# A new order of each engine's steps in a tuned f32 matrix product, with six sums a group on GpSimd where there were seven

## The chip, the cores and the metric

One core of a Trainium2 chip runs the whole program. The metric is the time of one execution on the device in microseconds; the profile is one profiled execution of the same program.

## The reference

```python
def reference(x, w):                     # x: 8 x 2048 x 2048, w: 2048 x 2048, float32
    cs = np.cumsum(x, axis=1)
    diff = cs - np.concatenate([zeros, cs[:, :-1, :]], axis=1)
    return np.matmul(diff, w).astype(np.float32)
```

The differences of a cumulated sum are the rows themselves, so the kernel computes x times w: 16384 x 2048 times 2048 x 2048.

## The kernel before

The 16384 rows are 128 row tiles of 128 rows. Each tile is loaded by SP in two halves into `F` (step `load`), its largest values are summed up by ScalarE (`weigh0`, `weigh1`, with an accumulator), GpSimd makes one number a row of it (`scale`, `unit`), VectorE the reciprocal (`recip`), ScalarE scales and narrows to fp16 (`narrow0`, `narrow1`), and SP turns it by DMA transposes (`turn0`, `turn1`) so that it can be TensorE's stationary operand. The weights stay in SBUF as fp16 blocks and differences of blocks.

The first 12 tiles go by separate code. The rest is 29 groups of four row tiles, g, h, k and l in the steps' names (tiles g, g+2, g+1, g+3). A group's product is a Strassen-Winograd scheme of two levels: seven products P1 to P7, of which P6 is done whole (eight parts `P6g.0` to `P6h.3`) and each other one is again seven quarters, `P1.p1` to `P1.p7`. A quarter is four matmuls of 128 x 128 by 128 x 512 into one PSUM bank; a group has 50 of them, 200 matmuls. Around them stand:

- large sums of row tiles on VectorE, 128 x 1024 fp16: `S1` to `S4` of each pair of tiles (`S1.g`, `S1.h` and so on);
- small sums, 128 x 512 fp16, four for each of P1, P2, P3, P4, P5 and P7: `P1.s1` to `P1.s4`, which feed p5, p6, p7 and p3. Those named in `ON_POOL` run on GpSimd, the others on VectorE;
- fills, 128 x 2048 fp16 on VectorE: differences of weights written into `flow` just before the quarter that uses them (`P1.fp4` before `P1.p4`, and so on; P7 has three);
- copies of PSUM banks to SBUF by ScalarE (`P1.cg`, `P1.ct`, `P7.c1` ...), sums of them back into banks by VectorE (`P1.m1`, `P7.a1`, `P7.a5g` ...), and the collection of results: `keep.C11g0` (ScalarE, the first part of a block of C into a buffer `c`), `add.C11g0.v` (VectorE, a further part added), `last.C12g0` (ScalarE, the scaling at the end), `put.C11g0` (SP, the store).

The order of it all is written out by hand in the string `ORDER`: some 270 steps, each with the number of groups it runs ahead. The loop at the end walks through it once for each group:

```python
for b in range(-early, len(groups) - late):
    for name, ahead in ORDER:
        if 0 <= b + ahead < len(groups):
            go_on(b + ahead, name)
```

Each engine issues its own steps in exactly this order (`after` chains them), and waits inside its queue for what a step needs from others. So the table fixes which step stands behind which on TensorE, VectorE, ScalarE, GpSimd and SP, and no step can overtake. SP's queue holds loads, turns and stores alike. In the last group the last quarters go by a table of their own (`END_ORDER`). In the first group P7 is done whole; `PLAINLY` says at which steps of the table its eight parts run. A few differences of weights that the scheme needs only once are made in the first group, at the steps named in `before`; `first(...)` is the one of its names that comes first.

Of the kernel before, what the change touches and what calls it, by code (L numbers as in the profile page):

```python
# [10 lines left out]
def kernel(  # L11
# [546 lines left out]

    def total(dst, p, q, op, pool=False):
        if pool:  # L560
            after("pool", lambda: nc.gpsimd.tensor_tensor(dst.all, p.all, q.all, op))  # L561
        else:
            after("dve", lambda: nc.vector.tensor_tensor(dst.all, p.all, q.all, op))  # L563
# [479 lines left out]

# [227 lines left out]
    ORDER = """
    P7.a5g+0 P7.p6+0 load.h+1 P7.c6+0 P7.p2+0 turn0.g+1 add.C22g0.x+0 keep.C12h1+0
    P5.p5+0 keep.C21g0+0 P7.a6+0 P5.s4+0 P3.s1+0 P7.p7+0 P7.c7+0 P4.p2+0 P7.a5h+0
    P3.s3+0 add.C21g0.x+0 narrow1.g+1 P5.p6+0 P7.a7h+0 P5.ct+0 put.C22g0+0 P3.p1+0
    weigh0.h+1 P5.m1+0 add.C12g0.q+0 weigh1.h+1 P7.p3+0 put.C21g0+0 P5.p7+0 P3.s2+0
    P3.s4+0 turn1.g+1 last.C12g0+0 P5.fp4+0 P5.m2+0 scale.h+1 recip.h+1 keep.C12h0+0
    unit.l+0 P5.p3+0 P3.p6+0 put.C12g0+0 P5.p4+0 P7.a7k+0 keep.C22g1+0 add.C22g1.x+0
    put.C22g1+0 P4.s2+0 P3.p3+0 P7.fp4+0 keep.C22h1+0 keep.C22h0+0 narrow0.h+1 load.k+1
    P4.s4+0 P4.p6+0 add.C12g1.z+0 P7.p4+0 add.C12h1.z+0 P3.p5+0 add.C22h1.x+0
    add.C12g1.q+0 add.C22h0.x+0 P4.p5+0 add.C12g1.e+0 P3.p4+0 P3.p7+0 keep.C21h1+0  # L1280
    narrow1.h+1 last.C12g1+0 P4.fp4+0 add.C12h0.z+0 add.C12h1.q+0 P4.s3+0 P4.p3+0
    add.C12h0.q+0 unit.g+1 add.C12h1.e+0 P2.p1+1 P1.p1+1 P4.p4+0 keep.C21g1+0 weigh0.k+1
    turn0.h+1 weigh1.k+1 scale.k+1 P1.s1+1 turn1.h+1 recip.k+1 P1.s3+1 P1.s2+1 unit.h+1
    add.C21g1.q+0 put.C12g1+0 last.C12h1+0 P1.cg+1 put.C22h0+0 P1.s4+1 P1.p5+1 P1.p6+1
    P2.s1+1 put.C22h1+0 put.C12h1+0 add.C21h1.e+0 narrow0.k+1 P1.ct+1 load.l+1 P1.m1+1
    last.C12h0+0 P4.p7+0 add.C21h1.q+0 P2.s2+1 narrow1.k+1 P1.p2+1 keep.C11g0+1
    turn1.k+1 P1.p7+1 P1.p3+1 keep.C21h0+0 unit.k+1 P2.cv+1 P1.fp4+1 P2.s4+1 P1.m2+1
    keep.C11g1+1 P2.p6+1 P1.p4+1 keep.C11h1+1 add.C21h0.x+0 P2.p5+1 add.C11g1.q+1
    P2.s3+1 weigh0.l+1 P2.fp4+1 turn0.k+1 add.C11h1.e+1 P2.p7+1 weigh1.l+1 scale.l+1
    put.C21h0+0 P2.p2+1 last.C21h1+0 recip.l+1 put.C12h0+0 add.C11h1.q+1 P2.p3+1 P2.p4+1  # L1290
    narrow0.l+1 add.C21g1.x+0 narrow1.l+1 put.C21h1+0 S1.g+1 keep.C11h0+1 S2.g+1
    add.C11g1.e+1 P5.p1+1 P5.cg+1 add.C11g0.v+1 P6g.1+1 turn0.l+1 P6g.2+1 P5.p2+1
    add.C11h0.q+1 turn1.l+1 load.g+2 S4.g+1 last.C21g1+0 P3.fp2+1 S1.h+1 P6g.3+1 P6g.0+1
    S2.h+1 last.C11h1+1 last.C11g1+1 P5.s1+1 keep.C22g0+1 weigh0.g+2 put.C21g1+0
    keep.C12g0+1 put.C11g0+1 put.C11h0+1 P5.s2+1 weigh1.g+2 P3.p2+1 P6h.2+1 scale.g+2
    P5.s3+1 S4.h+1 P6h.1+1 P7.fp5+1 S3.g+1 P6h.3+1 P6h.0+1 P4.s1+1 add.C12g0.z+1 S3.h+1
    keep.C12g1+1 P7.s1+1 P7.p1+1 put.C11h1+1 P7.s2+1 P4.p1+1 P7.c1+1 recip.g+2 P7.s3+1
    put.C11g1+1 P7.a1+1 P7.p5+1 P7.s4+1 narrow0.g+2 P7.fp7+1 P7.c5+1
    """
# [82 lines left out]
```

## Time and profile before

| what | us |
|---|---|
| median of 3 runs (lowest, highest) | 1457.22 (1456.07, 1460.31) |
| the profiled execution: its own time | 1458.12 |
| its span, first to last instruction | 1456.0 |
| TensorE busy in the span | 1430.1 (98%) |
| VectorE busy | 1391.5 (96%) |
| ScalarE busy | 1152.3 (79%) |
| GpSimd busy | 401.9 (28%) |
| mean granted TensorE clock | 1.000 |

The first 60 us load the weights, the 29 groups run from 171.2 us (the first matmul of group 0's `P1.p1`) to the end. The profile names lines, and most steps run through helpers: L592 is a quarter's matmuls, L573 those of a whole product, L563 a small or large sum on VectorE, L561 one on GpSimd, L958 a fill, L1055 and L1087 ScalarE's copies of banks, L1062 VectorE's sums into banks, L600 and L1117 `keep` and `last`, L603 and L1128 `add`, L614 `put`, L113 `load`, L185 `turn`, L125 `weigh`, L142 `scale`, L161 `unit`, L156 `recip`, L172 `narrow`. Which step a row is follows from its place in the order. A releaser in brackets is what ended the idle time before an instruction. TensorE's matmuls overlap in the rows: each is shown with 0.38 us, and in an unbroken run one starts 0.216 us after the other.

### The profile page before, as it was taken

What the parts mean: (1) busy time and instruction counts of PE and PEld (TensorE: products, weight loads), DVE (VectorE), ACT (ScalarE), POOL (GpSimd) and SP (SyncE); (2) the same over time, 40 slices, a digit from 0 to 9 for tenths busy, and PEclk for the clock granted to TensorE, in tenths of its full rate; (3) what the DMA queues carried; (4) which work ended last, traced back from release to release, by engine and by line L of the source; (5) the groups of instructions that cost most, each with busy time, mean ns of one, the idle gap of its engine ahead of it and who ended that gap; (6) DMA issues with size and microseconds to landing.
All of it is one profiled execution on the core that took longest, in us unless ns stands there. A gap on an engine that the chain in (4) does not pass through costs nothing. (4 is left out here: it accounts for less than half of the span.)

```text
span 1456.0 us, 21148 instructions
## 1 busy us (share of the span) xinstructions
PE 1430.1 (98%) x6561; PEld 637.2 (44%) x6567; DVE 1391.5 (96%) x2325; ACT 1152.3 (79%) x1782; POOL 401.9 (28%) x451
## 2 busy tenths in 40 slices
PE   8999999999999999999999999999999999999997
PEld 3444444444444444444444444444444444444443
DVE  7998879999999999999999999999999999999998
ACT  5887557888788888878888888888888888778882
POOL 0111122233232233232233232233232233232232
PEclk9999999999999999999999999999999999999999
DMA  9999849999889998899998889989889988899983
GB/s 355 365 243 301 209 144 229 257 229 249 219 237 245 241 234 254 234 232 251 234 238 248 236 241 256 237 232 252 237 240 250 242 226 249 233 233 256 237 235 122
DMA packets 377761, 351.65 MB, mean 242 GB/s; under 512 B 274800, under 2 KB 274800, under 8 KB 377520
## 3 DMA queue, kind: packets, MB, share of 16 engines
q1 hardware_dynamic: 377088, 348.47, 88.7%
q0 software_dynamic: 560, 1.84, 0.3%
q8 instruction: 51, 0.84, 0.3%
q14 instruction: 62, 0.51, 0.1%
HBM read 150.99 MB, written 134.22 MB: 196 GB/s over the span
## 5 line engine op out<-in xcount | busy, mean ns | idle before, releaser
L592 PE MATMUL b<-W,x 128*128 128x512 f16 x2116 | 509.8, 379 | 3.6 <-DVE x L563 1.2
L592 PEld LDWEIGHTS <-x 128*128 128x128 f16 x2936 | 285.4, 98 | 362.1 <-issue 18.7
L1128 DVE TENSOR_TENSOR c<-b,c 128x512 f32<-128x512 f32 x504 | 334.3, 689 | 4.5 <-PE b L592 3.6
L125 ACT ACTIVATE waste<-F 128x1024 uint8<-128x1024 f32 x246 | 260.7, 1060 | 94.8 <-DMA F<-in_x_dram 91.7
L592 PEld LDWEIGHTS <-inner 128*128 128x128 f16 x1984 | 192.1, 98 | 246.6 <-DVE inner L563 16.5
L592 PE MATMUL b<-W,inner 128*128 128x512 f16 x1168 | 295.0, 379 | 4.0 <-ACT c L1087 1.4
L172 ACT ACTIVATE F<-F,of 128x1024 f16<-128x1024 f32 x246 | 281.9, 1146 | 20.9 <-DVE of L156 19.0
L573 PE MATMUL b<-W,x 128*128 128x512 f16 x1248 | 285.7, 379 | 2.6 <-DVE x L563 2.3
L600 ACT ACTIVATE c<-b,of 128x512 f32<-128x512 f32 x268 | 176.2, 684 | 74.7 <-DMA out_dram<-c 42.9
L142 POOL TENSOR_SCALAR of<-of 128x1 f32<-128x1 f32 x112 | 59.9, 535 | 619.8 <-ACT waste L125 441.0
L603 DVE SCALAR_TENSOR_TENSOR c<-b,of,c 128x512 f32<-128x512 f32 x286 | 209.0, 746 | 10.3 <-PE b L592 4.2
L592 PE MATMUL b<-flow,x 128*128 128x512 f16 x812 | 208.3, 379 | 2.1 <-DVE of L156 1.1
L563 DVE TENSOR_TENSOR x<-x,x 128x1024 f16<-128x1024 f16 (+1 forms) x329 | 200.0, 616 | 7.7 <-DMA x<-F 4.9
L1062 DVE TENSOR_TENSOR b<-b,c 128x512 f32<-128x512 f32 x284 | 193.7, 694 | 7.9 <-ACT c L1087 3.4
L573 PEld LDWEIGHTS <-x 128*128 128x128 f16 x1248 | 121.5, 98 | 151.6 <-DVE x L563 7.8
L958 DVE TENSOR_TENSOR flow<-W 128x2048 f16<-128x2048 f16 x142 | 173.6, 1222 | 0.0
L600 ACT ACTIVATE c<-c,of 128x512 f32<-128x512 f32 x224 | 154.8, 715 | 10.1 <-DVE c L1128 7.7
L1117 ACT COPY c<-b 128x512 f32<-128x512 f32 x224 | 127.1, 581 | 18.3 <-DMA out_dram<-c 9.1
L561 POOL TENSOR_TENSOR x<-x,x 128x512 f16<-128x512 f16 x87 | 129.7, 1504 | 14.1 <-POOL x L561 7.6
L561 POOL TENSOR_TENSOR inner<-x,inner 128x512 f16<-128x512 f16 x58 | 95.7, 1651 | 118.3 <-PE b L592 118.3
L592 PE MATMUL b<-inner 128*128 128x512 f16 x472 | 121.1, 379 | 0.0
L561 POOL TENSOR_TENSOR inner<-inner,x 128x512 f16<-128x512 f16 x58 | 68.4, 1180 | 139.3 <-PE b L592 133.1
(77 smaller groups left out, 945.9 us busy)
## 6 DMA issues: line engine op xcount, KB each, us to landing
F<-in_x_dram SPq DMA_DIRECT2D x246, 512.0 KB, 5.7
out_dram<-c SPq DMA_DIRECT2D x492, 256.0 KB, 3.3
W<-in_w_dram SPq DMA_DIRECT2D x32, 512.0 KB, 9.5
W<-in_x_dram SPq DMA_DIRECT2D x16, 256.0 KB, 7.7
x<-F SPq DMA_TRANSPOSE x246, 3.6
out_dram<-o POOLq DMA_DIRECT2D x5, 256.0 KB, 4.0
out_dram<-o SPq DMA_DIRECT2D x5, 256.0 KB, 3.5
xP<-in_x_dram SPq DMA_DIRECT2D x1, 1024.0 KB, 5.4
```

The costliest lines, as they stand in the source:

```text
L125: lambda: nc.scalar.activation(waste, where[t][i], ABS, scale=1.0 / ROW, accum_out=sums_of[t][:, i : i + 1],),
L172: lambda: nc.scalar.activation(narrowed(t)[:, ds(i * NH, NH)], where[t][i], COPY, scale=s),
L561: after("pool", lambda: nc.gpsimd.tensor_tensor(dst.all, p.all, q.all, op))
L563: after("dve", lambda: nc.vector.tensor_tensor(dst.all, p.all, q.all, op))
L573: said = nc.tensor.matmul(to[n], a[k], b[k][:, n, :], start=(first and k == 0), stop=(k == KH - 1), skip_group_check=True,)
L592: said = nc.tensor.matmul(to, a[k], b[k], start=(first and k == 0), stop=(k == 3), skip_group_check=True)
L600: after("act", lambda: nc.scalar.activation(c, p, COPY, scale=u))
L603: after("dve", lambda: nc.vector.scalar_tensor_tensor(c, p, u, c, MUL, ADD))
L958: after("dve", lambda: nc.vector.tensor_tensor(in_twos(flow), x, y, op))
L1062: after("dve", lambda: nc.vector.tensor_tensor(t, p, s, ADD))
L1117: after("act", lambda: nc.scalar.copy(to, p))
L1128: after("dve", lambda: nc.vector.tensor_tensor(to, p, to, ADD))
```

## The change

Three things change: the table `ORDER`, the list of small sums that run on GpSimd, and the places of the first group's P7.

```diff
-    ON_POOL = "P2.s2 P2.s4 P3.s2 P4.s2 P4.s3 P4.s4 P5.s4".split()
+    ON_POOL = "P3.s1 P4.s2 P4.s3 P4.s4 P5.s3 P5.s4".split()
...
     ORDER = """
-    P7.a5g+0 P7.p6+0 load.h+1 P7.c6+0 P7.p2+0 turn0.g+1 add.C22g0.x+0 keep.C12h1+0
...
+    P6h.1+0 P6h.3+0 keep.C12g0+0 P5.s3+0 add.C12g0.z+0 put.C11h1+0 weigh0.g+1 weigh1.g+1
...
     PLAINLY = {
-        "P7.p1": ["P7g.0"],
-        "P7.p5": ["P7g.1"],
-        "P7.p6": ["P7g.2"],
-        "P7.p2": ["P7g.3"],
+        "P7.p2": ["P7g.0", "P7g.1", "P7g.2", "P7g.3"],
         "P7.a7k": ["P7h.0", "P7h.1"],
-        "P7.fp4": ["P7h.2"],
-        "P7.p4": ["P7h.3"],
+        "P7.fp4": ["P7h.2", "P7h.3"],
     }
```

The set of steps is the same. P2.s2, P2.s4 and P3.s2 move from GpSimd to VectorE, P3.s1 and P5.s3 from VectorE to GpSimd. On TensorE four quarters now stand between `P1.p1` and `P1.p5` (`P4.p5`, `P4.p3` and `P4.p4` of the group before, and `P2.p1`), where `P4.p4` alone stood. The three places that the prediction speaks of most, in the middle of the program:

VectorE around `S3.h`, before. Tiles x00 and x01 are the two halves of tile g, x10 and x11 of h, x20 and x21 of k, x30 and x31 of l. The rows are S3.g, P4.s1, add.C12g0.z, S3.h, P7.s1, P7.s2, recip.g, P7.s3 and P7.a1:

```order
L563 TENSOR_TENSOR x00_63<-x21_68,x00_63 128x1024
L563 TENSOR_TENSOR x20_67<-x31_70 128x512
L1128 TENSOR_TENSOR c5_767<-b7_791,c5_767 128x512
L563 TENSOR_TENSOR x10_65<-x31_70,x10_65 128x1024
L563 TENSOR_TENSOR inner_779<-x10_65 128x512
L563 TENSOR_TENSOR inner_779<-inner_779,x00_63 128x512
L156 RECIPROCAL of_6472<-of_6472 128x1
L563 TENSOR_TENSOR x10_65<-x00_63,x10_65 128x512
L1062 TENSOR_TENSOR b2_786<-b2_786,c4_763 128x512
```

and now, from S2.h and S3.g on: add.C11h0.q, add.C12g0.z, P5.s2, S4.h, P7.fp5, S3.h, recip.g, P7.s1, P4.s1, P7.s2:

```order
L563 TENSOR_TENSOR x10_65<-x30_69,x10_65 128x1024
L563 TENSOR_TENSOR x00_63<-x21_68,x00_63 128x1024
L603 SCALAR_TENSOR_TENSOR c2_755<-b7_791,of_6185,c2_755 128x512
L1128 TENSOR_TENSOR c0_747<-b5_789,c0_747 128x512
L563 TENSOR_TENSOR inner_779<-inner_779,x20_67 128x512
L563 TENSOR_TENSOR x11_66<-x11_66,x10_65 128x1024
L958 TENSOR_TENSOR flow_783<-W_58 128x2048
L563 TENSOR_TENSOR x10_65<-x31_70,x10_65 128x1024
L156 RECIPROCAL of_6499<-of_6499 128x1
L563 TENSOR_TENSOR inner_779<-x10_65 128x512
L563 TENSOR_TENSOR x20_67<-x31_70 128x512
L563 TENSOR_TENSOR inner_779<-inner_779,x00_63 128x512
```

The reciprocal of the next tile g stands ahead of P7.s1 and P7.s2 and no longer behind them; S3.g stands ahead of S4.h and the fill P7.fp5; P7.s2 is no longer right behind P7.s1, and P5.s3 has left for GpSimd.

SP behind the turns of tile l (x30, x31), before:

```order
L185 DMA_TRANSPOSE x30_69<-F_62 128x8x128
L185 DMA_TRANSPOSE x31_70<-F_62 128x8x128
L113 DMA F_62<-in_x_dram 128x1024 x2
L614 DMA out_0_dram<-c1_751 128x512
L614 DMA out_0_dram<-c4_763 128x512
```

and now:

```order
L185 DMA_TRANSPOSE x30_69<-F_62 128x8x128
L185 DMA_TRANSPOSE x31_70<-F_62 128x8x128
L614 DMA out_0_dram<-c4_763 128x512
L113 DMA F_62<-in_x_dram 128x1024 x2
L614 DMA out_0_dram<-c6_771 128x512
```

A store (put.C21h0 of the group before) now stands between the second turn and load.g.

GpSimd in one group, before: P2.s2, unit, P2.s4, two scales, P5.s4, P3.s2, scale, unit, P4.s2, P4.s4, P4.s3:

```order
L561 TENSOR_TENSOR inner_779<-inner_779,x01_64 128x512
L161 TENSOR_SCALAR of_3333<-of_3333,uw_59 128x1
L561 TENSOR_TENSOR inner_779<-x01_64,inner_779 128x512
L142 TENSOR_SCALAR of_3412<-of_3412 128x1
L142 TENSOR_SCALAR of_3488<-of_3488 128x1
L561 TENSOR_TENSOR inner_779<-x20_67,inner_779 128x512
L561 TENSOR_TENSOR inner_779<-inner_779,x01_64 128x512
L142 TENSOR_SCALAR of_3596<-of_3596 128x1
L161 TENSOR_SCALAR of_3412<-of_3412,uw_59 128x1
L561 TENSOR_TENSOR x20_67<-x20_67,x21_68 128x512
L561 TENSOR_TENSOR x30_69<-x21_68,x20_67 128x512
L561 TENSOR_TENSOR x31_70<-x21_68,x31_70 128x512
```

and now, from P5.s3 on: scale, P5.s4, P3.s1, P4.s2, scale, P4.s4, P4.s3:

```order
L561 TENSOR_TENSOR x30_69<-x20_67,x30_69 128x512
L142 TENSOR_SCALAR of_3888<-of_3888 128x1
L561 TENSOR_TENSOR inner_779<-x20_67,inner_779 128x512
L561 TENSOR_TENSOR inner_779<-x11_66 128x512
L561 TENSOR_TENSOR x20_67<-x20_67,x21_68 128x512
L142 TENSOR_SCALAR of_3947<-of_3947 128x1
L561 TENSOR_TENSOR x30_69<-x21_68,x20_67 128x512
L561 TENSOR_TENSOR x31_70<-x21_68,x31_70 128x512
```

The two sums of P2 are gone from it, P5.s3 has come ahead of scale.g, and P3.s1 takes the place of P3.s2.

More of the change, by code (lines that the diff above doesn't have):

```diff
@@ L1271 @@
     ORDER = """
-    P7.a5g+0 P7.p6+0 load.h+1 P7.c6+0 P7.p2+0 turn0.g+1 add.C22g0.x+0 keep.C12h1+0
[L1273 to L1295, printed above, removed]
@@ L1296 @@
-    P5.s3+1 S4.h+1 P6h.1+1 P7.fp5+1 S3.g+1 P6h.3+1 P6h.0+1 P4.s1+1 add.C12g0.z+1 S3.h+1
-    keep.C12g1+1 P7.s1+1 P7.p1+1 put.C11h1+1 P7.s2+1 P4.p1+1 P7.c1+1 recip.g+2 P7.s3+1
-    put.C11g1+1 P7.a1+1 P7.p5+1 P7.s4+1 narrow0.g+2 P7.fp7+1 P7.c5+1
+    P6h.1+0 P6h.3+0 keep.C12g0+0 P5.s3+0 add.C12g0.z+0 put.C11h1+0 weigh0.g+1 weigh1.g+1
+    put.C11g1+0 scale.g+1 P5.s2+0 P7.p1+0 S4.h+0 P7.c1+0 P7.fp5+0 S3.h+0 recip.g+1
+    P7.s1+0 P4.s1+0 narrow0.g+1 P7.s2+0 P7.s3+0 P4.p1+0 put.C11g0+0 P7.a1+0 P7.p5+0
@@ new lines @@
+    P7.s4+0 P7.fp7+0 P7.p6+0 keep.C12g1+0 put.C11h0+0 P7.c5+0 P7.p2+0 P5.p5+0 P7.a5g+0
+    P7.c6+0 add.C22g0.x+0 keep.C12h1+0 P7.a5h+0 P7.a6+0 P7.p7+0 load.h+1 weigh0.h+1
+    P7.c7+0 put.C22g0+0 P7.a7h+0 P4.p2+0 keep.C21g0+0 P5.s4+0 P5.p6+0 add.C21g0.x+0
+    P5.ct+0 P3.s1+0 P5.m1+0 P7.p3+0 turn0.g+1 P3.p1+0 P5.p3+0 P4.s2+0 narrow1.g+1
+    P5.p7+0 P3.s2+0 P3.s3+0 weigh1.h+1 P4.p6+0 scale.h+1 P3.s4+0 keep.C22g1+0
+    add.C12g0.q+0 P5.fp4+0 put.C21g0+0 P3.p3+0 P5.m2+0 add.C22g1.x+0 keep.C12h0+0
@@ new lines @@
+    P7.a7k+0 P5.p4+0 add.C12g1.z+0 P3.p6+0 last.C12g0+0 keep.C22h0+0 recip.h+1 P3.p5+0
+    keep.C22h1+0 P7.fp4+0 P4.s4+0 add.C12g1.q+0 P3.p4+0 turn1.g+1 put.C12g0+0
+    add.C22h1.x+0 narrow0.h+1 add.C12g1.e+0 keep.C21h1+0 put.C22g1+0 add.C12h1.e+0
+    P7.p4+0 P4.s3+0 add.C22h0.x+0 load.k+1 P3.p7+0 turn0.h+1 P4.fp4+0 narrow1.h+1
+    last.C12g1+0 weigh0.k+1 weigh1.k+1 scale.k+1 P1.p1+1 unit.g+1 P4.p5+0 turn1.h+1
+    add.C12h1.z+0 P4.p3+0 add.C12h1.q+0 unit.h+1 P4.p4+0 add.C12h0.z+0 P2.p1+1
+    last.C12h1+0 P1.s1+1 put.C22h1+0 add.C12h0.q+0 P1.s2+1 keep.C21g1+0 P1.p5+1
@@ new lines @@
+    recip.k+1 put.C12g1+0 P2.s1+1 add.C21h1.e+0 put.C22h0+0 P1.cg+1 P1.s4+1 last.C12h0+0
+    P1.ct+1 P1.p6+1 add.C21g1.q+0 put.C12h1+0 load.l+1 narrow0.k+1 P1.m1+1 P1.p2+1
+    P4.p7+0 keep.C11g0+1 P1.s3+1 P2.s2+1 add.C21g1.x+0 add.C21h1.q+0 turn0.k+1 P1.fp4+1
+    narrow1.k+1 P1.p3+1 turn1.k+1 P2.s4+1 P2.cv+1 keep.C21h0+0 add.C21h0.x+0 P2.p6+1
+    P1.p7+1 P1.m2+1 P2.p2+1 P2.p5+1 weigh0.l+1 keep.C11g1+1 weigh1.l+1 scale.l+1
+    add.C11g1.q+1 P2.s3+1 put.C12h0+0 P1.p4+1 P2.p7+1 keep.C11h1+1 recip.l+1
@@ L1299 @@
+    add.C11h1.e+1 last.C21h1+0 P2.p3+1 S1.g+1 S2.g+1 unit.k+1 add.C11h1.q+1 P2.fp4+1
+    P5.p1+1 add.C11g1.e+1 put.C21h1+0 S4.g+1 narrow0.l+1 narrow1.l+1 P6g.1+1 P6g.0+1
+    P5.cg+1 turn0.l+1 keep.C11h0+1 P2.p4+1 last.C11h1+1 add.C11g0.v+1 last.C21g1+0
+    P5.p2+1 turn1.l+1 keep.C22g0+1 P6g.3+1 P3.fp2+1 put.C21h0+0 S1.h+1 load.g+2 P5.s1+1
+    S2.h+1 P6g.2+1 P3.p2+1 put.C21g1+0 last.C11g1+1 S3.g+1 add.C11h0.q+1 unit.l+1
+    P6h.2+1 P6h.0+1
     """
```

## The prediction

> **What bounds the kernel now.** I read the page's busy times first, then the windows cut at the starts of groups of four row tiles, then the waits of single engines, then the timeline of one undisturbed and one disturbed group.
>
> ```profile
> span 1456.0 us, 21148 instructions
> PE 1430.1 (98%) x6561; PEld 637.2 (44%) x6567; DVE 1391.5 (96%) x2325; ACT 1152.3 (79%) x1782; POOL 401.9 (28%) x451
> ...
> 171.20:217.30 46.10, 43.33 (x197) 18.90 (x196) 36.93 (x56) 23.66 (x38) 10.79 (x10) 1.00 0.57 163
> 217.30:263.10 45.80, 43.92 (x201) 19.32 (x200) 44.93 (x77) 36.50 (x59) 14.19 (x15) 1.00 0.92 230
> 263.10:1358.60 1095.50, 1089.51 (x5001) 485.76 (x5000) 1069.33 (x1827) 904.34 (x1427) 332.89 (x375) 1.00 0.91 240
> 791.10:920.80 129.70, 129.70 (x601) 58.62 (x600) 128.05 (x221) 108.70 (x171) 39.97 (x45) 1.00 0.90 244
> 834.40:877.60 43.20, 43.20 (x201) 19.51 (x200) 42.65 (x74) 36.18 (x58) 13.40 (x15) 1.00 0.91 244
> 659.40:703.60 44.20, 43.68 (x201) 19.25 (x200) 42.73 (x74) 36.26 (x57) 13.26 (x15) 1.00 0.93 235
> 1402.60:1456.00 53.40, 45.44 (x206) 19.78 (x204) 48.70 (x79) 26.09 (x40) 11.85 (x12) 0.99 0.54 164
> ```
>
> The columns of a window are its length, then the busy time of PE, PEld, DVE, ACT and POOL, the granted clock, the DMA share and GB/s. The group at 834.40 is the yardstick: TensorE never pauses, and 200 matmuls take 43.20 us, so one quarter (four matmuls) takes 0.864. VectorE works 42.65 of these 43.20 us, so it has 0.55 us to spare in a group. The window from 791.10 holds three such groups in a row; cut at their first matmuls in the timeline, 8 of 25 groups are within 0.15 us of this bare time. The 25 groups from 263.10 to 1358.60 take 1095.50 where 25 x 43.20 = 1080.0 would do: 15.5 us are lost, more than the busy column shows (1095.50 - 1089.51 = 6.0), since each pause is partly covered by the modelled end of the matmul before it. The first two groups lose 91.9 - 86.4 = 5.5 more. That is all an order can win in the steady part. In the last group VectorE is the longer queue (48.70 against 45.44).
>
> Who is late is told by VectorE's waits in those 25 groups:
>
> ```profile
> DVE of L156 <- POOL of L142: 6.9, 27, 0.7
> DVE x L563 <- DMA x<-F: 4.5, 7, 1.1
> DVE b L1062 <- ACT c L1087: 3.4, 7, 0.9
> DVE inner L563 <- DMA x<-F: 1.6, 5, 0.5
> ```
>
> They sum to 16.4 us, about the 15.5 lost. One case, in the group at 659.40, VectorE's row ahead of TensorE's:
>
> ```profile
> 677.68 1.42 DVE L563 TENSOR_TENSOR x<-x,x 128x1024 f16<-128x1024 f16 x2 [0.93 <-DMA x<-F]
> ...
> 679.16 3.63 PE L573 MATMUL b<-W,x 128*128 128x512 f16 x16 [0.43 <-DVE x L563]
> ```
>
> The transpose of tile l lands 0.93 late, S1.h waits, P6h waits for S2.h, and this group is 1.0 us longer than the yardstick. With so little idle time VectorE can't catch up within the group, so a late arrival is paid nearly in full.
>
> **The change, part by part.** *One more small sum on VectorE.* P2.s2, P2.s4 and P3.s2 come to VectorE, P3.s1 and P5.s3 leave it: seven GpSimd sums become six in each of 29 groups. The price is in these rows:
>
> ```profile
> 853.01 0.42 DVE L563 TENSOR_TENSOR inner<-x 128x512 f16<-128x512 f16 x1
> 853.46 0.42 DVE L563 TENSOR_TENSOR inner<-inner,x 128x512 f16<-128x512 f16 x1
> 853.80 1.02 DVE L563 TENSOR_TENSOR x<-x,x 128x512 f16<-128x512 f16 x2
> ```
>
> The third starts 0.34 after the second, which it doesn't read. The second, which reads the first's result, starts 0.45 after it. So an extra sum takes 0.34 of the queue, and a sum right behind its own source 0.11 more. Of such neighbours a group has five before (S2.g, S2.h, P5.s2, P7.s1, P7.s2) and three now (S2.g, P5.s1, C12h1.q): 0.34 - 2 x 0.11 = 0.12 a group. The spare 0.55 hides it in an undisturbed group. Where something is late it counts; with 25 - 8 = 17 groups longer than the yardstick I charge 17 x 0.12 = 2.0 us. If the cover were gone everywhere it would be 29 x 0.12 = 3.5.
>
> *GpSimd loses a sum.* It is busy 28%, and no wait of TensorE names it. Worth 0.
>
> *The order of TensorE's quarters.* P1.p5 now has four quarters between itself and P1.p1 (P4.p5, P4.p3, P4.p4, P2.p1) where it had one, so P1.s1 seems to have 2.6 us more time. But the three P4 quarters and P2.p1 came earlier before, and VectorE's P1.s1 stands behind the same additions. Against the total work done nothing moves: 0.
>
> *S3.g of the first group.* This group's P7 is a whole product, and its first part sat right behind P6h:
>
> ```profile
> 190.00 3.62 PE L573 MATMUL b<-W,x 128*128 128x512 f16 x16
> 194.53 1.04 PE L573 MATMUL b<-W,x 128*128 128x512 f16 x4 [0.91 <-DVE x L563]
> ```
>
> Sixteen matmuls from 190.00 end their issue at 193.46, so 1.07 us are lost waiting for S3.g. Now all four parts stand at P7.p2, behind P4.p1, and S3.g stands ahead of S4.h. I take 1.1 us as won (at least 0, if S3.g is as late as before; at most the 5.5 us of the first two groups).
>
> *recip.l and recip.k.* These are the 6.9 us in 27 waits above, 42% of all. recip.k now stands behind P1.s2 rather than directly behind P1.s1, and the loads that feed k come no later against it. If this kind goes, 42% of 15.5 = 6.5 us goes. The landings (4.5 + 1.6) have no more room than before: S1.h still follows the second turn of l with nothing but additions and one fill between. I leave them. Bounds for this term: 0 to 15.5; I take 6.5, less the 2.0 above.
>
> *recip.g in front of P7.s1, and a put in front of load.g.* This speaks against the change. Rows of the undisturbed group, by time:
>
> ```profile
> 849.51 1.01 SPq L113 DMA_DIRECT2D F<-in_x_dram  x2
> 850.57 3.37 SPq L614 DMA_DIRECT2D out_dram<-c  x5
> ...
> 856.23 1.06 ACT L125 ACTIVATE waste<-F 128x1024 uint8<-128x1024 f32 x1
> 857.47 0.78 POOL L142 TENSOR_SCALAR of<-of 128x1 f32<-128x1 f32 x1 [12.09 <-DMA out_dram<-c]
> 858.13 0.42 DVE L563 TENSOR_TENSOR inner<-x 128x512 f16<-128x512 f16 x1
> ...
> 858.61 1.53 PEld L592 LDWEIGHTS <-inner 128*128 128x128 f16 x8 [0.19 <-DVE inner L563]
> 858.93 0.16 DVE L156 RECIPROCAL of<-of 128x1 f32<-128x1 f32 x1
> ```
>
> load.g is issued at 849.51, weigh1.g waits for it, scale.g ends at 857.47 + 0.78 = 858.25, and P7.p5 starts at 858.61 behind P7.s1. Before, recip.g comes after P7.s1 and P7.s2, so it could be 0.7 late at no cost. Now it stands ahead of P7.s1, and P7.s1 has to start by 858.61 - 0.05 - 0.42 = 858.14, the reciprocal 0.08 earlier, at 858.06. P1.p5 to P7.p5 is 26 quarters in both orders, and ScalarE's queue from P1.ct to narrow1.l keeps its list but for one entry: narrow0.k now stands behind P1.ct, where last.C12h0 stood.
>
> ```profile
> 836.30 1.03 PE L592 MATMUL b<-W,inner 128*128 128x512 f16 x4
> ...
> 836.75 1.14 ACT L172 ACTIVATE F<-F,of 128x1024 f16<-128x1024 f32 x1
> 837.80 0.56 ACT L1055 COPY c<-b 128x512 f32<-128x512 f32 x1
> 838.26 0.72 ACT L600 ACTIVATE c<-c,of 128x512 f32<-128x512 f32 x1
> 838.89 1.13 ACT L172 ACTIVATE F<-F,of 128x1024 f16<-128x1024 f32 x1
> 839.93 1.24 ACT L600 ACTIVATE c<-b,of 128x512 f32<-128x512 f32 x2
> ```
>
> By the starts, narrow0.k (1.05) for last.C12h0 (0.63) makes the chain 0.42 longer; but P1.ct, which began at 837.80, need no longer wait for narrow0.k behind the end of P1.p5 at 837.33, 0.47 less. The two cancel. So scale.g is late by the 858.25 - 858.06 = 0.19, and by a put that now stands on SP between the second turn of l and load.g, 3.37 / 5 = 0.67: 0.86 us a group. Yet scale.g takes not 0.78 but on the mean of all its kind
>
> ```profile
> L142 POOL TENSOR_SCALAR of<-of 128x1 f32<-128x1 f32 x112 | 59.9, 535 | 619.8 <-ACT waste L125 441.0
> ```
>
> 0.535. Whether SP's issue or the data set load.g's landing the trace doesn't show (the DMA share is 0.91), so of the put's 0.67 I take the middle between none and all: 0.19 + 0.33 - 0.25 = 0.27. A group that is already late at an earlier place doesn't pay it again; I charge the eight groups at the bare time and as many that the recip term frees, 16 x 0.27 = 4.3 us. The bounds are 0 and 25 x 0.86 = 21.5.
>
> *GpSimd sums beside VectorE's f16 sums.* One collision is in the trace, in the last group:
>
> ```profile
> 1434.40 1.16 POOL L561 TENSOR_TENSOR x<-x,x 128x512 f16<-128x512 f16 x1
> 1434.92 0.92 DVE L563 TENSOR_TENSOR inner<-x,inner 128x512 f16<-128x512 f16 x1
> 1435.76 1.21 DVE L958 TENSOR_TENSOR flow<-W 128x2048 f16<-128x2048 f16 x1
> ```
>
> P3.s4 takes 0.92 instead of 0.42 while GpSimd's sum is under way. So a collision costs 0.50 and the kernel before has one; removing it wins 0.5 at most. The Trainium skill (SBUF — State Buffer, "Who interferes with whom") says that a VectorE instruction with two SBUF inputs and a GpSimd instruction that reads SBUF contend, and that whichever comes second waits for the whole of the first. The trace agrees here with 0.92; by that rule any new overlap would cost VectorE up to GpSimd's 1.16, and the sum would be 25 x 0.5 = 12.5 us worse if one arose in each group. I find no certain one in the new order and take 0; its upper end is a rival.
>
> *The tail.* VectorE's last group grows by 0.12 and nothing covers it: 0.1.
>
> **The sum.** -1.1 - 6.5 + 2.0 + 4.3 + 0.1 = -1.2 us. The profiled execution took 1458.12 (span 1456.0 and 2.1 around it), 0.9 above the median of 1457.22; so that execution would come to 1456.9, and the median to 1456.0. That is 0.1%, within the 0.3% (4.4 us) which a measurement of this kernel can just tell from no change.
>
> **Rivals.** *Most late arrivals are swallowed (faster).* In the new order P7.fp4 has three quarters between its release by P5.p4 and P7.p4 instead of two, and P5.m1 feeds P5.p3 only after two other quarters. If the chains have slack at most places, two thirds of 15.5 go, 10.3, with 1.1 of the start and no new price: 1457.2 - 11.4 = 1445.8. For it: eight groups already run at the bare 43.2, so no fixed term stands in the way. Against it: the landings depend on transfers whose DMA share is 0.91 in either order.
>
> *The recip.g chain binds in every group (slower).* Price 0.6 in all 25 groups instead of 0.27 in 16: 25 x 0.6 - 1.1 - 4.5 + 0.1 = +9.5, or 1466.7. It decides from (4.4 + 5.5) / 25 = 0.40 a group on. For it: the 0.78 of the undisturbed group, and 0.25 MB more queued ahead of load.g. Against: the mean of 0.535, and that late groups don't pay twice.
>
> *GpSimd's P5.s3 holds P5.s2 (slower).* P5.s3 may begin when S2.h ends, behind S3.g's reads, and P5.s2 follows on VectorE three steps after S3.g began, 1.8 us. GpSimd would need 0.6 of waiting and 1.16 of work, also 1.8. If it loses that race in each group: 25 x 0.5 - 1.1 - 4.5 + 0.1 = +7.0, or 1464.2. By the skill's rule above this race is real; the trace shows only the one collision.
>
> *It changes nothing.* The stated aim, no GpSimd sum just ahead of a small VectorE sum, already holds in 28 of 29 groups; a time equal to before lies inside my forecast.
>
> **How the numbers follow.** The forecast near no change 0.37 (its own range 1453 to 1461); swallowed arrivals 0.35; recip.g chain 0.18; GpSimd race 0.10. Hence faster 0.35, same 0.37, slower 0.28. The range goes from 1446, the time of the fast rival, to 1468, just past the slow one; the outer tails hold about 0.1 each.
>
> **What would show it.** Right: the window of 25 groups near 1091 to 1095; waits "DVE of L156 <- POOL of L142" below 6.9; the first PE pause at 194 gone; small sums beside GpSimd all at 0.42. Wrong on recip.g: that wait rises above 10 and sits ahead of an "inner<-x" sum, with TensorE pausing 0.3 or more at P7.p5 in most groups. Wrong on the race: VectorE f16 sums of 0.9. Wrong on the fast side: most groups at 43.2.

## The result: 2.7% slower, and the profile after

The changed kernel takes 1496.60 us (median of 4 runs, 1495.16 to 1499.30) against 1456.64 for the kernel before in the same runs: a ratio of 1.0272, 95% interval 1.0248 to 1.0296, or 40 us. The prediction said 1456.0 with a range up to 1468. It was wrong by far.

The page's head, and the windows cut at the first matmuls of P1.p1 (columns as in the prediction: length, PE, PEld, DVE, ACT, POOL, granted clock, DMA share, GB/s). The first two are the first two groups, then come the 25 groups from the third on, one group among them, and the last group:

```profile
span 1494.2 us, 21188 instructions
PE 1443.4 (97%) x6567; PEld 632.4 (42%) x6567; DVE 1412.6 (95%) x2354; ACT 1143.9 (77%) x1782; POOL 352.7 (24%) x422
...
170.17:217.84 47.67, 43.42 (x189) 18.56 (x188) 33.88 (x54) 21.12 (x35) 9.87 (x8) 0.96 0.56 156
217.84:264.89 47.05, 44.24 (x202) 19.23 (x200) 45.66 (x79) 36.89 (x59) 11.23 (x14) 1.00 0.81 217
264.89:1391.19 1126.30, 1099.48 (x5002) 480.82 (x5001) 1089.30 (x1849) 896.43 (x1425) 290.04 (x350) 1.00 0.85 234
895.04:940.46 45.42, 43.95 (x201) 19.23 (x200) 43.59 (x75) 35.82 (x58) 11.59 (x14) 1.00 0.82 231
1437.19:1494.20 57.01, 48.94 (x218) 20.77 (x216) 52.45 (x85) 29.03 (x46) 10.97 (x12) 0.99 0.52 158
```

The 25 groups take 1126.30 instead of 1095.50, so 30.8 of the span's 38.2 us (1494.2 - 1456.0) are lost there, 1.2 in each group. The shortest of them takes 44.5; none is near 43.2 any more. The first group's window holds 189 matmuls where it held 197 (the order moves two quarters behind the cut, 8 x 0.216 = 1.7 us), so like for like it is 3.3 us longer and not 1.6. The last group's 3.6 more are for the greater part no loss of their own: P1.p1 now stands three quarters (2.6 us) earlier in a group's work, so that work which used to lie ahead of the cut lies behind it.

VectorE's waits in these 25 groups, and its fills `flow<-W` there, after:

```profile
DVE of L156 <- POOL of L142: 30.7, 50, 2.1
DVE x L563 <- DMA x<-F: 1.7, 5, 0.5
```

```profile
L958 DVE TENSOR_TENSOR flow<-W 128x2048 f16<-128x2048 f16 x125 | 174.7, 1398 | 0.0
```

and the same fills in the 25 groups of the kernel before:

```profile
L958 DVE TENSOR_TENSOR flow<-W 128x2048 f16<-128x2048 f16 x125 | 152.8, 1223 | 0.0
```

Two prices stand out. VectorE waits 30.7 us for GpSimd's `scale` where it waited 6.9; by the rows 25.3 of these are recip.g, once in every group. And 125 fills take 21.9 us more, all of it in one of the five fills of a group. Together that is 45.7 us. The late turns and the copies of ScalarE that VectorE waited for before (4.5 + 1.6 + 3.4) have shrunk to 1.7, which leaves 38; the 7 us between this and the 30.8 are less than VectorE's former idle time of 0.55 a group, 25 x 0.55 = 13.8.

One group of the changed kernel by time. First around recip.g:

```profile
876.62 0.68 DVE L563 TENSOR_TENSOR x<-x,x 128x1024 f16<-128x1024 f16 x1
876.71 1.06 ACT L125 ACTIVATE waste<-F 128x1024 uint8<-128x1024 f32 x1 [0.56 <-DMA F<-in_x_dram]
877.96 0.30 POOL L142 TENSOR_SCALAR of<-of 128x1 f32<-128x1 f32 x1 [3.57 <-ACT waste L125]
878.29 0.16 DVE L156 RECIPROCAL of<-of 128x1 f32<-128x1 f32 x1 [0.98 <-POOL of L142]
878.37 0.41 DVE L563 TENSOR_TENSOR inner<-x 128x512 f16<-128x512 f16 x1
878.83 1.04 PE L592 MATMUL b<-flow,inner 128*128 128x512 f16 x4 [0.61 <-DVE inner L563]
```

S3.h ends at 877.30, and then VectorE stands still for 0.98 us: the half tile that ScalarE weighs (L125) landed only at 876.7, and GpSimd's `scale` follows the weighing. P7.s1 and with it TensorE's P7.p5 wait behind the reciprocal. Then the fill P7.fp4 of the same group, 12.97 us behind P7.s1:

```profile
891.24 3.25 POOL L561 TENSOR_TENSOR x<-x,x 128x512 f16<-128x512 f16 x2 [3.76 <-PE b L592]
891.34 2.14 DVE L958 TENSOR_TENSOR flow<-W 128x2048 f16<-128x2048 f16 x1
```

GpSimd's P4.s4 starts 0.10 ahead of it (the row joins P4.s4, 1.15 us, and P4.s3). The fill takes 2.14 instead of 1.22: the sum is done at 892.39, and the fill ends 1.09 behind it. The same pair in the kernel before, in the group that the prediction used as its yardstick:

```profile
870.35 2.25 POOL L561 TENSOR_TENSOR x<-x,x 128x512 f16<-128x512 f16 x1 [0.28 <-POOL x L561]
870.36 1.22 DVE L958 TENSOR_TENSOR flow<-W 128x2048 f16<-128x2048 f16 x1
```

Here they start 0.01 us apart, the fill has its usual 1.22, and it is GpSimd's sum that takes 2.25 instead of 1.16, where nobody waits for it. So the two collided in the kernel before as well. Which of them waits has changed.

### The profile page after: what moved, and what is told of

Same layout as the page of the kernel before. It is cut to its first block, busy times and chain, and to the rows that moved or that the text cites. A ratio compares the mean times of both kernels' runs of the same rounds, so it can differ in the third digit from the quotient of the medians.

```text
span 1494.2 us, 21188 instructions
## 1 busy us (share of the span) xinstructions
PE 1443.4 (97%) x6567; PEld 632.4 (42%) x6567; DVE 1412.6 (95%) x2354; ACT 1143.9 (77%) x1782; POOL 352.7 (24%) x422
## 4 chain that ended last, share of the span: by engine, by line
DVE 39%; DMA 17%; PE 17%; issue 13%; ACT 10%; SPq 2%; POOL 1%; DVEq 0%; ACTq 0%
DMA F<-in_x_dram 12%; DVE c L1128 12%; PE b L592 9%; DVE flow L958 8%; DVE b L1062 7%; PE b L573 6%; DVE c L603 5%; ACT waste L125 4%; DVE x L563 4%; DVE inner L563 3%; ACT F L172 2%; PE b L289 2%; ACT b L1055 2%; ACT c L600 1%; DMA out_dram<-c 1%
## 5 line engine op out<-in xcount | busy, mean ns | idle before, releaser
L592 PE MATMUL b<-W,x 128*128 128x512 f16 x2116 | 518.6, 379 | 3.9 <-DVE c L603 2.0
L125 ACT ACTIVATE waste<-F 128x1024 uint8<-128x1024 f32 x246 | 260.7, 1060 | 69.8 <-DMA F<-in_x_dram 68.1
L592 PEld LDWEIGHTS <-inner 128*128 128x128 f16 x1984 | 186.7, 98 | 291.2 <-DVE inner L563 73.4
L573 PE MATMUL b<-W,x 128*128 128x512 f16 x1248 | 287.3, 381 | 3.8 <-ACT c L1117 2.6
L561 POOL TENSOR_TENSOR x<-x,x 128x512 f16<-128x512 f16 x116 | 170.9, 1484 | 365.0 <-DVE x L563 229.5
L958 DVE TENSOR_TENSOR flow<-W 128x2048 f16<-128x2048 f16 x142 | 196.7, 1385 | 0.0
L563 DVE TENSOR_TENSOR x<-x,x 128x1024 f16<-128x1024 f16 (+1 forms) x300 | 187.6, 633 | 3.1 <-DMA x<-F 1.7
L1117 ACT COPY c<-b 128x512 f32<-128x512 f32 x224 | 130.4, 583 | 45.0 <-DVE c L603 33.2
L142 POOL TENSOR_SCALAR of<-of 128x1 f32<-128x1 f32 x112 | 38.0, 339 | 536.4 <-ACT waste L125 536.4
L600 ACT ACTIVATE c<-c,of 128x512 f32<-128x512 f32 x224 | 159.3, 724 | 1.1 <-DVE c L1128 1.1
L592 PE MATMUL b<-inner 128*128 128x512 f16 x472 | 116.6, 379 | 0.0
L1055 ACT COPY b<-b 128x512 f32<-128x512 f32 x87 | 50.4, 579 | 66.4 <-DVE c L1128 62.0
L1087 ACT COPY c<-b 128x512 f32<-128x512 f32 x112 | 65.4, 585 | 24.7 <-PE b L592 23.4
```

Of the source, the lines that this page charges most:

```text
L125: lambda: nc.scalar.activation(waste, where[t][i], ABS, scale=1.0 / ROW, accum_out=sums_of[t][:, i : i + 1],),
L573: said = nc.tensor.matmul(to[n], a[k], b[k][:, n, :], start=(first and k == 0), stop=(k == KH - 1), skip_group_check=True,)
L592: said = nc.tensor.matmul(to, a[k], b[k], start=(first and k == 0), stop=(k == 3), skip_group_check=True)
L600: after("act", lambda: nc.scalar.activation(c, p, COPY, scale=u))
L958: after("dve", lambda: nc.vector.tensor_tensor(in_twos(flow), x, y, op))
L1117: after("act", lambda: nc.scalar.copy(to, p))
```

## The experiments

Theory: two prices on VectorE's queue, each paid in nearly every group. (a) A race: whichever of the fill and the GpSimd sum comes second waits for the first, and a few hundredths of a microsecond decide. (b) The chain from recip.l over the turns, the store put.C21h0 and load.g to recip.g is longer than VectorE's work between the two. Rivals: one price that causes the other, VectorE's longer queue alone, or transfers.

### The race, from both sides

In the changed kernel, `recip.h+1` moved from in front of `P7.fp4+0` to right behind it:

```diff
-    ... keep.C22h0+0 recip.h+1 P3.p5+0 keep.C22h1+0 P7.fp4+0 P4.s4+0 ...
+    ... keep.C22h0+0 P3.p5+0 keep.C22h1+0 P7.fp4+0 recip.h+1 P4.s4+0 ...
```

> The changed kernel with one reciprocal (recip.h, 0.08 us of VectorE's queue) moved from in front of the fill P7.fp4 to behind it; nothing else. Theory of the race: the fill then starts about 0.02 instead of 0.09 after GpSimd's P4.s4 and wins, as in the kernel before, where the offset is 0.01; the fill takes 1.22 instead of 2.14, P4.s4 takes 2.2 instead of 1.16, and the time falls by 27 x 0.92 = 25 us, to about 1472. If 0.02 is still too late, the fill stays at about 2.1 and the time at 1496. Rival, the fill is slow because of something other than who starts first: no change, 1495 to 1498.

Measured: 1480.79 us, 15.8 less, ratio to the kernel before 1.0163 (1.0143 to 1.0184). The pair now:

```profile
930.44 2.25 POOL L561 TENSOR_TENSOR x<-x,x 128x512 f16<-128x512 f16 x1 [3.77 <-PE b L592]
930.46 1.22 DVE L958 TENSOR_TENSOR flow<-W 128x2048 f16<-128x2048 f16 x1
```

An instruction of 0.08 us taken from in front of the fill hands the wait back to GpSimd in 23 of 25 groups. It won 16 us and not 25, since recip.g's waits grew (27.3 us in the 25 groups against 25.3) and late turns show again that lateness had covered (S1.g, S1.h and P1.s1 wait 6.3 us together, against 1.8).

The counterpart in the kernel before, one reciprocal too many in front of the fill:

```diff
+    spare = const.tile([P, 1], f32, name="spare")
...
+        if name == "P7.fp4" and groups[i].more:
+            after("dve", lambda: nc.vector.reciprocal(spare, uw))
```

> The kernel before with one extra reciprocal of 128 x 1 to a spare tile in front of the fill P7.fp4 in each steady group; its result is not used. It costs VectorE's queue 0.08 us a group by itself, at most 29 x 0.08 = 2.3 us. Theory of the race: the fill now starts 0.09 after GpSimd's P4.s4 instead of 0.01 and waits for it, 2.14 instead of 1.22; VectorE's queue grows from 42.7 to 43.7 us, over TensorE's 43.2, and a group that took 43.8 on the mean takes 44.3 to 44.8: 1470 to 1485. Rival, the fill's slowness belongs to the other order and not to who starts first: 1457 to 1459.

Measured: 1477.69 us against 1457.79 of the kernel before in the same runs, ratio 1.0142 (1.0125 to 1.0160). An extra instruction that costs 2.3 us at most by itself costs 20:

```profile
925.32 3.25 POOL L562 TENSOR_TENSOR x<-x,x 128x512 f16<-128x512 f16 x2 [0.29 <-POOL x L562]
925.33 0.15 DVE L1343 RECIPROCAL spare<-uw 128x1 f32<-128x1 f32 x1
925.40 2.15 DVE L959 TENSOR_TENSOR flow<-W 128x2048 f16<-128x2048 f16 x1
```

The order of the rest is that of the kernel before; only the start of the fill has moved by 0.08, and 22 of 25 fills are hit. TensorE pays at once, by 18.9 us of pauses in the 25 groups at P7.p4, the quarter that reads the fill. This settles (a).

### recip.g's chain

The reciprocal later, in the changed kernel (the narrowing that reads it goes behind P7.c5):

```diff
-    ... S3.h+0 recip.g+1 P7.s1+0 P4.s1+0 narrow0.g+1 P7.s2+0 P7.s3+0 P4.p1+0 ... P7.c5+0 P7.p2+0 ...
+    ... S3.h+0 P7.s1+0 P4.s1+0 P7.s2+0 P7.s3+0 recip.g+1 P4.p1+0 ... P7.c5+0 narrow0.g+1 P7.p2+0 ...
```

> The changed kernel with the reciprocal of the next tile g three small sums later on VectorE (behind P7.s3), and the narrowing that needs it behind P7.c5. Theory of two prices (the wait of recip.g and the fill P7.fp4 behind a GpSimd sum are paid one beside the other on VectorE's queue): the wait of about 1.02 us a group goes, the fill stays at 2.14, a group takes about 44.1 instead of 45.1, and the time is 1496.6 - 27 x 1.1 = about 1467. Rival, one price (the fill is hit only because the wait holds VectorE back against TensorE): the fill falls to 1.22 as well, groups go to 43.2 to 43.9, and the time is 1450 to 1460. Rival, the longer VectorE queue alone (42.82 us of work in 43.2): no gain over 5 us.

Measured: 1466.87 us, 29.7 less, ratio 1.0066 (1.0051 to 1.0081), as the theory of two prices had it. recip.g's waits in the 25 groups fall from 25.3 to 2.2 us, and the fill is still hit in 18 of 25: the race is a price of its own. Of the 29.7 us, 20.0 are won in the 25 groups; the first group falls from 47.7 to 43.6 us, of which more below.

What makes the chain long? put.C21h0 in front of the turns of l, where SP has time. The kernel before had it on that side of the turns too, further ahead:

```diff
-    P5.cg+1 turn0.l+1 ... P3.fp2+1 put.C21h0+0 S1.h+1 load.g+2
+    P5.cg+1 put.C21h0+0 turn0.l+1 ... P3.fp2+1 S1.h+1 load.g+2
```

> The changed kernel with the store put.C21h0 moved the other way on SP, in front of the two turns of l instead of between them and load.g, so that load.g follows the second turn directly and no buffer comes free later. If the store's issue of 0.6 to 0.67 us stands in the chain that ends in recip.g, the wait of recip.g falls from 1.0 to about 0.4 and the time to 1496.6 - 27 x 0.6 = about 1480. If load.g's landing is set by the data on their way, the wait stays at about 1.0 and the time at 1494 to 1498.

Measured: 1474.40 us, 22.2 less, ratio 1.0116 (1.0100 to 1.0131). VectorE's waits for `scale` over the whole program, first in this run, then in the changed kernel:

```profile
DVE of L156 <- POOL of L142: 12.7, 53, 0.9
```

```profile
DVE of L156 <- POOL of L142: 34.3, 55, 2.1
```

recip.g's part falls from 25.3 to 5.7 us in 25 groups, 0.8 a group; what stays is mostly 0.20 each. But the store had made the load later by twice that. The chain in the group shown above, whose weighing starts at 876.71, first the changed kernel:

```profile
866.02 2.61 SPq L185 DMA_TRANSPOSE x<-F  x2
868.69 0.57 SPq L614 DMA_DIRECT2D out_dram<-c  x1
869.36 0.88 SPq L113 DMA_DIRECT2D F<-in_x_dram  x2
```

and a group of this run, up to recip.g:

```profile
810.13 2.68 SPq L185 DMA_TRANSPOSE x<-F  x2
812.91 1.01 SPq L113 DMA_DIRECT2D F<-in_x_dram  x2
...
819.08 1.06 ACT L125 ACTIVATE waste<-F 128x1024 uint8<-128x1024 f32 x1 [0.73 <-DMA F<-in_x_dram]
...
820.32 1.38 POOL L142 TENSOR_SCALAR of<-of 128x1 f32<-128x1 f32 x1 [1.70 <-ACT waste L125]
820.85 0.69 DVE L563 TENSOR_TENSOR x<-x,x 128x1024 f16<-128x1024 f16 x1
821.74 0.17 DVE L156 RECIPROCAL of<-of 128x1 f32<-128x1 f32 x1 [0.20 <-POOL of L142]
```

From the first turn's issue to the weighing it is 10.69 us in the changed kernel and 8.95 here. On the mean of the 25 groups, counted from recip.l, load.g's second half is issued 0.4 us earlier without the store in front of it, takes 5.7 us instead of 6.9 to land, and scale.g starts 1.6 us earlier. So SP's issue is the smaller part of what the store costs the load, and the longer way of the data is the larger; why their way is longer is not shown. VectorE feels 0.8 of the 1.6 us, and the 0.20 that stays is no late load: scale.g starts at 820.32 and ends at 821.70, 0.16 behind S3.h (820.85 to 821.54). It takes 1.38 us beside VectorE's fill P7.fp5 and S3.h, and 0.30 in the changed kernel, where VectorE stands still. In 20 of the 25 groups it ends 0.16 to 0.17 behind S3.h.

The other part of the chain by itself, in the kernel before: recip.g in front of P7.s1 and nothing else.

```diff
-    keep.C12g1+1 P7.s1+1 P7.p1+1 put.C11h1+1 P7.s2+1 P4.p1+1 P7.c1+1 recip.g+2 P7.s3+1
+    recip.g+2 keep.C12g1+1 P7.s1+1 P7.p1+1 put.C11h1+1 P7.s2+1 P4.p1+1 P7.c1+1 P7.s3+1
```

> The kernel before with one reciprocal moved: recip.g in front of P7.s1, as in the changed kernel, instead of behind P7.s2. From recip.l to recip.g the chain of narrowing, turns, load, weighing and scale takes about 14.1 us in the changed kernel, while VectorE has 12.9 us of work between the two in this order. Theory of the chain: recip.g waits 0.8 to 1.1 us in most groups, P7.s1 and P7.p5 with it; VectorE's queue comes to 43.6 us and more, and the time is 1470 to 1482. Fill P7.fp4 starts 0.08 earlier and still wins. By the 0.19 us that the prediction worked out from one undisturbed group, the wait is 0.2 to 0.3 and the time 1457 to 1463.

Measured: 1459.91 against 1457.55, ratio 1.0017 (1.0004 to 1.0029), 2.4 us. My expectation of 1470 and more fell. The wait is 0.19 in most groups, the number that the prediction had worked out from one group, but the rows show another reason for it:

```profile
812.94 0.69 DVE L563 TENSOR_TENSOR x<-x,x 128x1024 f16<-128x1024 f16 x1
813.04 0.73 POOL L142 TENSOR_SCALAR of<-of 128x1 f32<-128x1 f32 x1 [12.13 <-DVE c L1128]
813.81 0.16 DVE L156 RECIPROCAL of<-of 128x1 f32<-128x1 f32 x1 [0.19 <-POOL of L142]
813.89 0.41 DVE L563 TENSOR_TENSOR inner<-x 128x512 f16<-128x512 f16 x1
```

S3.h, the first row, ends at 813.63 and scale.g at 813.77. In 23 of the 25 groups scale.g ends 0.15 us behind S3.h, whether it starts just ahead of S3.h or 0.5 us into it. So GpSimd's `scale` is held up until VectorE's sum is done, and the 0.19 is the end of that collision, not a load that lands late. It was so in the prediction's own group of the kernel before, where S3.h ends at 858.09 and scale.g at 858.25:

```profile
857.41 0.68 DVE L563 TENSOR_TENSOR x<-x,x 128x1024 f16<-128x1024 f16 x1
```

A wait of 0.19 a group costs little where VectorE has 0.55 to spare. The 1.0 of the changed kernel, where the store makes the load late, is more than it has.

The store on the other side, put.C21h0 behind load.g in the changed kernel:

```diff
-    ... put.C21h0+0 S1.h+1 load.g+2 P5.s1+1 ...
+    ... S1.h+1 load.g+2 put.C21h0+0 P5.s1+1 ...
```

> The changed kernel with the store put.C21h0 behind load.g on SP again, where the kernel before had it; recip.g stays in front of P7.s1. The prediction charged half of an SP issue of 0.67 us for it. If the store's whole 0.67 us stands in the chain that ends in recip.g, the wait of recip.g falls from 1.0 to about 0.35 a group and the time to 1496.6 - 27 x 0.67 = 1478.5; if half, 1487; if the landing of load.g is set by the data on their way and not by SP, the wait stays at 1.0 and the time at 1495 to 1498.

Measured: 1571.53 us, ratio 1.0798 (1.0779 to 1.0818), 75 us slower still, which none of the cases foresaw. ScalarE's waits name the cause:

```profile
ACT c L1117 <- DMA out_dram<-c: 94.5, 25, 5.3
```

keep.C12g0 writes into the buffer that put.C21h0 empties, and the store behind the load lands too late for it; VectorE's add.C12g0.z then waits 2.9 us a group, and so does TensorE at P7.p5. That the store must not stand behind load.g is shown; the run tells nothing on the 0.67. The expectation was also wrong on the kernel before: there put.C21h0 stood ahead of the turns of l, not behind load.g.

### Both prices away, and what is left

> The changed kernel with both edits, recip.g behind P7.s3 and recip.h behind the fill. Theory of two prices: both go, TensorE bounds again, groups take 43.2 to 43.9, and the time is 1450 to 1460, about the kernel before or up to 7 us better. If VectorE's three more sums are what costs, it stays above 1475. If the wait of recip.g only moves to another place (TensorE waits for the turns of the next tile g), it is 1465 to 1480.

Both edits of above, recip.g behind P7.s3 and recip.h behind the fill: 1465.38 us (1461.30 to 1469.35), ratio 1.0057 (1.0038 to 1.0075). The sum of two prices was too simple: less than 2 us below recip.g alone. The expected 1450 to 1460 was missed, and the rival in which recip.g's wait only moves (1465 to 1480) is not borne out: recip.g waits 2.2 us in the 25 groups, TensorE shows no wait for a turn, and VectorE's waits for late turns there are 5.6 us, 6.1 in the kernel before. Since recip.g no longer ties VectorE to TensorE at P7.p5, the fill comes between 0.12 ahead of P4.s4 and 0.71 behind it, and 6 of 25 are still hit.

> The changed kernel with put.C21h0 in front of the turns of l and recip.h behind the fill; recip.g stays in front of P7.s1. If the two prices (the store in front of load.g, 0.8 us a group of recip.g's wait; the fill behind GpSimd's sum, 0.92) are the change's whole loss, VectorE's queue is 42.8 us of work and 0.7 of waits (recip.g 0.28, recip.l 0.28, add.C12h1.q 0.19), 43.5 to 43.7 a group, and the time is 1452 to 1459. If the fill is still hit in half of the groups, since recip.g no longer ties VectorE to TensorE, it is 1462 to 1470.

put.C21h0 in front of the turns and recip.h behind the fill: 1460.18 us against 1457.49, ratio 1.0023 (1.0010 to 1.0035). Two small moves bring back 36.4 of the 40 us; alone they brought 22.2 and 15.8. That is the change's loss, but for 2.7 us. In the profiled run the 25 groups take 1095.3 us, as in the kernel before (1095.5), so the rest lies in the groups ahead of them and behind them:

```profile
262.10:1357.39 1095.29, 1086.90 (x5001) 484.05 (x5000) 1069.61 (x1849) 895.75 (x1425) 312.63 (x350) 1.00 0.87 240
```

> The changed kernel with put.C21h0 in front of the turns of l, recip.g behind P7.s3 and recip.h behind the fill. If what was left in the run with two edits (1465.4, 8.8 above the kernel before) is lateness of loads behind that store, it goes, and the time is 1450 to 1457. If it is VectorE's queue of 42.8 us with the waits of recip.l and add.C12h1.q, 0.47 us a group, or fills that are hit in some of the groups, it is 1460 to 1467, as with two edits.

All three edits: 1454.74 against 1457.49, ratio 0.9979 (0.9970 to 0.9988), 2.8 us faster than the kernel before. 23 of 25 fills win, and the 25 groups are back at 43.8 us each:

```profile
259.48:1353.98 1094.50, 1086.37 (x5002) 486.21 (x5001) 1071.27 (x1851) 892.79 (x1426) 310.02 (x350) 1.00 0.87 241
```

This kernel has the new list of GpSimd sums. VectorE's one more sum a group therefore costs nothing that shows here.

Giving a sum back to GpSimd did not help the kernel with two edits:

```diff
-    ON_POOL = "P3.s1 P4.s2 P4.s3 P4.s4 P5.s3 P5.s4".split()
+    ON_POOL = "P2.s4 P3.s1 P4.s2 P4.s3 P4.s4 P5.s3 P5.s4".split()
```

> The kernel with both edits (recip.g behind P7.s3, recip.h behind the fill), and P2.s4 on GpSimd again, as in the kernel before: seven sums on GpSimd. VectorE's queue becomes 0.34 us a group shorter. If VectorE's queue bounds what is left (42.8 us of work and 0.35 of waits in 43.2), groups lose up to 0.34 us less: 1465.4 - 25 x 0.34 = about 1457, or below with the late fills gone. If the rest comes from transfers, 1462 to 1468. If GpSimd's sum falls beside one of VectorE's small sums, those show 0.9 and nothing is won.

Measured: 1467.34, ratio 1.0071 (1.0053 to 1.0089). No small sum was hit, but another fill was, P1.fp4 (`flow<-W,S`), which P2.s4 now precedes by 0.1:

```profile
797.46 1.15 POOL L561 TENSOR_TENSOR inner<-x,inner 128x512 f16<-128x512 f16 x1 [4.46 <-PE b L592]
797.57 2.13 DVE L958 TENSOR_TENSOR flow<-W,S 128x2048 f16<-128x2048 f16 x1
```

The mean of its 29 instances is 1.998 us, where it was 1.216 with the two edits alone.

Two more moves in the kernel with two edits, recip.l behind add.C11h1.e and add.C12h0.z between add.C12h1.z and add.C12h1.q:

```diff
-    recip.l+1 add.C11h1.e+1 ... add.C12h1.z+0 P4.p3+0 add.C12h1.q+0 unit.h+1 P4.p4+0 add.C12h0.z+0
+    add.C11h1.e+1 recip.l+1 ... add.C12h1.z+0 P4.p3+0 add.C12h0.z+0 add.C12h1.q+0 unit.h+1 P4.p4+0
```

> The kernel with both edits (recip.g behind P7.s3, recip.h behind the fill), and two more: recip.l one addition later (behind add.C11h1.e), since it waits 0.24 in every group, and add.C12h0.z between add.C12h1.z and add.C12h1.q, which stand right behind each other and cost 0.10. If VectorE's queue bounds what is left, a group loses 0.3 us more and the time is 1465.4 - 25 x 0.3 = about 1458, or down to 1452 if the late fills go too. If the later recip.l makes the turns of l late, S1.h waits more instead and the time stays at 1462 to 1468.

Measured: 1483.79, ratio 1.0188 (1.0173 to 1.0203), 18 us worse. add.C11h1.e, now first, waits for ScalarE's keep in 25 of 25 groups (9.4 us together), S1.h waits for late turns in 9 groups instead of 6, and the fill is hit 15 times instead of 6. recip.l's wait had covered another one. Which of the two moves turns the fill over is not shown.

### The first group's P7

> The kernel before with the new places of the first group's P7 alone (P7g.0 to P7g.3 at P7.p2, P7h.2 and P7h.3 at P7.fp4). The prediction's term is -1.1 us, with bounds 0 and -5.5. In the runs with recip.g later the first group took 43.55 us against 46.07 in the kernel before, which points to -2.5; if the first part still waits at its new place, as it did for 2.76 us in the changed kernel, it is +1 to +2.

The kernel before with the new `PLAINLY` alone: 1454.64 against 1456.91, ratio 0.9984 (0.9973 to 0.9995). The first two groups take 89.7 instead of 91.9 us. The -2.5 of the expectation compared unlike windows: the 43.55 us hold 189 matmuls and the 46.07 hold 197, which leaves about -0.8.

> The kernel before with the new places of the first group's P7 and recip.k behind P1.s3 instead of directly behind P1.s1, where it waits 0.2 in 22 of 25 groups (4.5 us together). If VectorE's lateness is what disturbed groups pay for, the 4.5 us come back in those groups (17 of 25, so about 3 us) beside the 1 to 2.5 of P7: 1451 to 1454. If a group's lateness comes from transfers alone, only P7's part comes: 1454 to 1456.

With recip.k behind P1.s3 as well: 1455.82, ratio 0.9996 (0.9985 to 1.0007). recip.k waits 4.3 us in all where it waited 4.5: it is late by its data, and the move brings nothing.

In the changed kernel the same places cost instead of win. P7g.0 stops behind its third matmul:

```profile
196.48 1.15 ACT L172 ACTIVATE F<-F,of 128x1024 f16<-128x1024 f32 x1 [4.62 <-DVE of L156]
197.53 1.05 ACT L1117 COPY c<-b 128x512 f32<-128x512 f32 x2
198.15 4.87 PE L573 MATMUL b<-W,x 128*128 128x512 f16 x14 [2.60 <-ACT c L1117]
```

It waits for a bank that ScalarE has to copy out, the copy stands behind narrow0.g, and that waits for recip.g. With recip.g and narrow0.g later this group takes 43.55 us.

## Why the prediction was wrong, step by step

- **GpSimd sums beside VectorE's f16 sums** ("I find no certain one in the new order and take 0"): this step failed, and it is half of the loss. The prediction looked only at VectorE's late instructions and at small sums, and so it counted one collision in the kernel before. There are 29 P4.s4, and in the 25 groups each collided with the fill and lost. A GpSimd row of 2.25 beside others of 1.16, in the yardstick group itself, would have shown it. P5.s4 too took 1.7 to 2.0 us in every group. The place to check was the order from P7.s1 to P7.fp4 on VectorE against that from P7.p5 to P5.p4 on TensorE. Measured in place of the 0: about 0.9 us in each of the 25 groups, 21.9 us of fills. The rule of the Trainium skill that it cited (SBUF — State Buffer, "Who interferes with whom", the second waits for the whole of the first) holds for the fill as it stands: 2.14 us, of which 1.05 are the rest of GpSimd's sum. The prediction had even worked out 12.5 us for one new overlap a group, and gave it no place in the sum.
- **recip.g** ("0.19 + 0.33 - 0.25 = 0.27", 4.3 us in 16 groups): this step failed too. The place was right, the working and the size were not; measured are 1.0 in each of the 25 groups, 25.3 us of waits. The 0.19 was read as a late load and added to the put's price, but it is the end of scale.g's collision with S3.h. The put was priced at one issue on SP, 0.67, and then halved because the trace did not tell; it made the load 1.6 us later, the greater part of it while the data were on their way. That the two parts unhalved, 0.86, come near the measured 1.0 is luck. The sum was also made with the groups that are late anyway left out; every group pays. The rival that binds in every group had that right, and was too cheap with 0.6.
- **recip.l and recip.k** (-6.5): fell. recip.k's wait is gone from VectorE's list, but recip.l now waits in every group (5.4 us in 25 groups, 2.3 before).
- **S3.g of the first group** (-1.1): right in sign, -2.3 by itself in the time. In the changed kernel it became a loss through narrow0.g, which the prediction had not followed to ScalarE's next copy.
- **One more small sum on VectorE** (+2.0): not seen in a time; the kernel with three edits has it, and TensorE's new order, and is faster than the kernel before.
- **The rival of P5.s3 and P5.s2**: right kind, wrong pair. P5.s2 stays at 0.41 in all groups.
- **What bounds**: right. VectorE's 0.55 us of spare time hid the reciprocal's 0.19 almost whole where it came alone, and could not hide 0.92 and 1.0.
- **The range** ended at 1468, as each rival was one mechanism; here two of one sign came together, and one of them had no rival of its own.

## What to carry to other kernels

Where two engines hold each other up, list the collisions in which the other engine loses too: they cost nothing now, but here a shift of less than 0.1 us turned them over, and then each cost most of the length of the other's instruction in nearly every pass of the loop. Where VectorE was tied to TensorE by a wait, the offset was nearly the same in every pass, so the race was lost almost always or almost never; leave a margin there, as the kernel with three edits does with 0.1 us, or move the instruction. And price a store in front of a load by when the load lands, not by the store's issue. A wait that is the same to 0.01 us in most groups, while what it waits for starts at any time, pointed at a collision here and not at a late transfer.
